# Scaling seven of eight token tiles on VectorE before a plain transpose, and leaving the learned tokens out of the query projections, in one encoder layer on a Trainium2 core

## The chip, the cores and the metric

The program runs on one core of a Trainium2 chip. It uses the core's TensorE (matmuls, in the profile PE, with the weight loads shown apart as PEld), VectorE (DVE), ScalarE (ACT), GpSimd (POOL) and SyncE (SP), which issues nearly all DMAs. The metric is the device time of one execution in microseconds (us); less is better.

## What is computed

The layer takes 1024 tokens of width 1024, puts 16 learned ("meta") tokens in front, and works on 1040 rows. Cut to what the change touches, the reference is:

```python
def rmsnorm(x, w):
    y = xf * lax.rsqrt(jnp.mean(xf * xf, axis=-1, keepdims=True) + RMS_EPS)
    return (y * w)

h = rmsnorm(h_res, norm1_w)                       # 1040 rows
proj = h @ w_in                                   # q | k | v | z | beta, a | sc_b, sc_c, sc_x | gates
o_dn = gated_deltanet_bidir(q, k, v, z, ...)      # conv of 5 taps over tokens on q, k, v; scans both ways
merged = sigmoid(gate_a) * y_a + sigmoid(gate_b) * y_b
h_res = h_res + merged @ w_out
h2 = rmsnorm(h_res, norm2_w)                      # the second norm
gu = h2 @ w_gate_up
h_res = h_res + (silu(gu[..., :D_FF]) * gu[..., D_FF:]) @ w_down
out = rmsnorm(h_res, final_norm_w)[:, N_META:]    # the learned tokens are dropped
```

All of it is float32. A row of the output belongs to one of the 1024 tokens. The learned tokens reach those rows through keys and values of the scans, while a query is used in its own row alone; a query row is a sum of projected rows from two tokens back to two tokens ahead.

## The kernel before, in words

Activations lie transposed, feature by token, so that each weight block of 128 columns can be the stationary operand and the tokens stream past it. To keep float32 accuracy every operand is held as a high and a low part, and a product is three matmuls: high by high, high by low, low by high.

**Stage 1, projections and scans (0 to about 1090 us).** 69 weight blocks of `w_in`, of 128 columns each, are projected as "units" (`u_qkv`, `u_short`, `u_gate`, `u_z`). A unit streams the tokens in chunks through `dense_steps` (lines 287 to 297): 8 steps of 3 matmuls per chunk. `u_qkv(h, i, w)` projects keys (i = 0), queries (i = 1) or values (i = 2) of head h over the chunks `QCH` of 336, 320 and 384 tokens. ACT copies a chunk into the row buffer `raw`, and into `dst` times the middle conv tap. `conv_job` (lines 309 to 326) then adds the other four taps on DVE, in two halves of 520 tokens (`HALF`), with tanh on ACT between. Beside the units run the per-head streams (decay, norm of q and k, triangular inverse, scan), written as generators.

What sets the order in this stage is a planner inside the program: `T` holds a planned time for each engine, `pe(ns)`, `V(n)` and `A(n)` add planned costs as the code is written out, and `run_streams` and `pump` decide by `T` after each dense step which stream or conv step is written next. The order is then fixed; the engines execute it as it stands. A change in any planned cost therefore can move all that is written later in this stage.

**Stage 2 (about 1090 to 1310 us)** is the two branch projections; it is untouched.

**Stage 3, output projection and second norm (about 1310 to 1413 us).** A loop over eight token tiles t of 128 tokens (lines 1261 to 1288). Each does 48 matmuls of 512 columns (`b`, `wh`, `wl`; lines 1273 to 1275), DVE adds the residual (line 1276), ACT squares the row (line 146), DVE makes `rs` = 1/rms in a chain of one-column instructions (`rms_scale`, `rsqrt`), and `hn` = row times norm weight (line 1284; line 1281 for the last tile). `norm_T(t, rs, hn)` then brings the tile to feature-by-token form. It is called one iteration late, so that TensorE does another tile's 48 matmuls in between; the last tile's call comes after the first matmuls of stage 4. In `norm_T`, `hn` is the stationary operand and `diag`, the identity times `rs`, is the moving one: the matmul (line 166) transposes and scales at once. Eight such matmuls a tile; ACT and DVE then split the result into the operands of stage 4 (`b_hl`, and for tiles 4 to 7 sums and differences `m32`, in rows called `al`).

Outside stage 1 a scheduler orders each engine's queue when the program is built.

**Stage 4, the feed-forward (about 1397 us to the end)**: a two-by-two block scheme with seven products in place of eight, called `product` (lines 1333 to 1335). Its moving operands T2 (in rows `mA`), T3, T4 and B22 (in rows `b`) are split at its start by lines 86 and 87 from the results of stage 3, some in a piece of 3 tiles (1536 elements) and a piece of 1 tile.

Of the kernel before, what the change touches and what calls it, by code (L numbers as in the profile page):

```python
# [8 lines left out]
F32 = mybir.dt.float32  # L9
# [3 lines left out]
ALU = mybir.AluOpType  # L13
# [3 lines left out]
P = 128  # L17
D = 1024
KT = 8
SEQ = 1024  # L20
META = 16
# [16 lines left out]
def encoder_layer(ctx: ExitStack, tc: tile.TileContext, x, meta, norm1_w, w_in,  # L38
                  dn_conv_w, A_log, dt_bias, dn_norm_w, sc_conv_w, w_bdn, w_bsc,
                  w_out, norm2_w, w_gu, w_down, final_w, out):  # L40
    nc = tc.nc
    x, out = x[0], out[0]
# [12 lines left out]
    def uid(s):  # L55
        cnt["n"] += 1
        return f"{s}_{cnt['n']}"

    def s4(n=1024):
        return tp.tile([P, 1024], F32, tag="s4", name=uid("s4"), bufs=4)[:, :n]  # L60

    def psm():
        return ps.tile([P, 512], F32, tag="m", name=uid("pm"), bufs=3)

    def psd():
        return ps.tile([P, 512], F32, tag="e", name=uid("pe"), bufs=2)
# [6 lines left out]
    def psany():  # L73
        rot["i"] += 1
        return (psm, psm, psm, psd, psd, pss, pss, pss)[rot["i"] % 8]()

    ident = keep.tile([P, P], F32, name="ident")
    make_identity(nc, ident)

    mm = nc.tensor.matmul  # L80

    def transpose(dst, src, n=P):
        nc.tensor.transpose(dst, src, ident[:n, :n])

    def split(hi, lo, src):
        nc.scalar.copy(hi, src)  # L86
        nc.vector.tensor_tensor(out=lo, in0=src, in1=hi.bitcast(F32), op=ALU.subtract)  # L87
# [64 lines left out]
    def sub(out, a, b):  # L152
        nc.vector.tensor_tensor(out=out, in0=a, in1=b, op=ALU.subtract)

    def norm_T(t, rs, hn):

        diag = tp.tile([P, P], F32, tag="diag", name=uid("diag"), bufs=1)
        nc.vector.tensor_scalar(out=diag, in0=ident, scalar1=rs, scalar2=None, op0=ALU.mult)
        c = slice(t % 4 * P, t % 4 * P + P)
        pts = []  # L160
        for g in range(2):
            pt = psany().rearrange("p (k t) -> p k t", k=4)
            pts.append(pt)
            for k in range(4):
                kk = 4 * g + k
                mm(pt[:, k], hn[:, kk * P:(kk + 1) * P], diag, start=True, stop=True)
            if t < 4:
                split(*(m[:, :, c] for m in mov[("B11", "B21")[g]]), pt)
        if t < 4:
            return  # L170
        b11h, b11l = (m[:, :, c].bitcast(F32) for m in mov["B11"])
        b22, t1, t2, t3 = (m[:, :, c] for m in m32)
        nc.scalar.copy(b22, pts[1])
        sub(t1, pts[0], b11h)
        sub(t1, t1, b11l)
        sub(t2, b22, t1)
        sub(t3, b22, pts[0])
# [34 lines left out]

    HALF = ((0, 520), (520, 520))
    QCH = ((0, 336), (336, 320), (656, 384))

# [5 lines left out]
    def on(e, ns, ready=0.0):  # L223

        T[e] = max(T[e], ready, T["pe"]) + ns
        return T[e] + TOPE
# [5 lines left out]
    def V(n, kind=0):  # L232
        return on("dve", (68 + 1.042 * n, 130 + 1.042 * n, 130 + 0.52 * n)[kind])

    def A(n):
        return on("act", 144 + 0.834 * n)
# [19 lines left out]
    def enqueue(lane, gen):  # L256
        j = Job(gen)
        if not lanes[lane]:
            spent[lane] = max(spent[lane], min(spent.values()))
        lanes[lane].append(j)  # L260
        return j
# [26 lines left out]
    def dense_steps(po, w, xx, t0, n):  # L288
        wh, wl = w
        xh, xl = xx  # L290
        t0 += C0
        for k in range(KT):
            mm(po[:, :n], wh[:, k], xh[:, k, t0:t0 + n], start=(k == 0), stop=False)  # L293
            mm(po[:, :n], wh[:, k], xl[k][:, t0:t0 + n], start=False, stop=False)  # L294
            mm(po[:, :n], wl[:, k], xh[:, k, t0:t0 + n], start=False, stop=(k == KT - 1))  # L295
            pe(3 * (n / 2.4 + 13))
            yield
# [3 lines left out]
    def row_buffer():  # L301
        if len(raws) >= 2:
            force(raws[-2])
        return d1.tile([P, 1044], F32, tag="ra", name=uid("ra"), bufs=2)

    def half_buffer():
        return d1.tile([P, 520], F32, tag="rb", name=uid("rb"), bufs=3)

    def conv_job(raw, dst, col, st_, key):

        for h0, hn in HALF:
            acc = dst[:, h0:h0 + hn]
            while st_["rows"] < h0 + hn + 4:
                yield max(T["pe"], T["dve"]) + 300
            for t in (0, 1, 3, 4):
                nc.vector.scalar_tensor_tensor(out=acc, in0=raw[:, h0 + t:h0 + t + hn], scalar=wc[:, t, col:col + 1],  # L316
                                               in1=acc, op0=ALU.mult, op1=ALU.add)
                V(hn, 1)
                yield T["dve"] + DEP
            th = half_buffer()  # L320
            nc.scalar.activation(th[:, :hn], acc, AF.Tanh)
            on("act", 0, T["dve"] + HOP)
            yield A(hn)
            nc.vector.scalar_tensor_tensor(out=acc, in0=th[:, :hn], scalar=1.0, in1=acc, op0=ALU.add, op1=ALU.mult)
            t = V(hn, 1)
        yield t

    def u_qkv(h, i, w):

        st_ = heads[h]  # L330
        if i == 0:
            st_["kq"] = d1.tile([P, 2, L], F32, tag="kq", name=uid("kq"), bufs=3)
            st_["vT"] = d1.tile([P, L], F32, tag="vT", name=uid("vT"), bufs=2)
        col = (8 + h, h, 16 + h)[i]
        dst = (st_["kq"][:, 0], st_["kq"][:, 1], st_["vT"])[i]
        raw = None
        sub = {"rows": 0}
        for ci, (t0, n) in enumerate(QCH):
            po = psm()
            yield from dense_steps(po, w, hx, t0, n)  # L340
            if raw is None:
                raw = row_buffer()
                nc.gpsimd.memset(raw[:, 0:2], 0.0)
                nc.gpsimd.memset(raw[:, L + 2:L + 4], 0.0)
            nc.scalar.copy(raw[:, 2 + t0:2 + t0 + n], po[:, :n])
            nc.scalar.activation(dst[:, t0:t0 + n], po[:, :n], AF.Copy, scale=wc[:, 2, col:col + 1])  # L346
            A(n)
            A(n)
            sub["rows"] = 2 + t0 + n if ci < 2 else L + 4
            if ci == 1:  # L350
                job = enqueue("conv", conv_job(raw, dst, col, sub, "t"))
                raws.append(job)
        key = ("tk", "tq", "tv")[i]

        def watch():
            return job.done
        st_[key] = watch
# [580 lines left out]
    with tc.tile_pool(name="st", bufs=1) as st:  # L938
# [6 lines left out]
        raw = st.tile([P, KT, 32], F32, name="wba_raw")  # L945
        rows = st.tile([P, 2, P], F32, name="rows")
        wc = c1.tile([P, 5, 24], F32, name="wc")
        for ts, ci in (((0,), None), ((1, 2), 0), ((3, 4, 5), 1), ((6, 7, 8), 2)):
# [5 lines left out]
            for i, t in enumerate(ts):  # L954
                p = P if t < 8 else META
                xr = xs[t] = st.tile([P, D], F32, tag="xr", name=uid("xr"), bufs=9)
# [10 lines left out]
            if ci == 0:  # L967
# [8 lines left out]
                pt = psd()  # L976
                transpose(pt[:, :120], rows[:120, 0], 120)
                nc.scalar.mul(wc.rearrange("p k t -> p (k t)"), pt[:, :120], 0.5)
                pt = psd()
# [3 lines left out]
            for i, t in enumerate(ts):  # L983
                p = P if t < 8 else META
                hn = xs[t]
                nc.vector.scalar_tensor_tensor(out=hn[:p], in0=hn[:p], scalar=ss[:p, 1, i:i + 1], in1=w1row[:p],
                                               op0=ALU.mult, op1=ALU.mult)
                for g in range(2):
                    pt = psany().rearrange("p (k t) -> p k t", k=4)
                    for k in range(4):  # L990
                        kk = 4 * g + k
# [7 lines left out]
            if ci is None:  # L999
                continue  # L1000
            t0, n = QCH[ci]
            if ci == 1:
# [34 lines left out]
        for d in range(2):  # L1037
            h0 = d * 64
            oth = 64 - h0
            nc.gpsimd.tensor_scalar(out=U2[d][h0:h0 + 64], in0=U[d][h0:h0 + 64], scalar1=-1.0,  # L1040
                                    scalar2=None, op0=ALU.add)
# [141 lines left out]
    tp = ctx.enter_context(tc.tile_pool(name="tp", bufs=1))  # L1183
# [54 lines left out]
    for j in range(KT):  # L1238
# [10 lines left out]
        raw = s4(D)  # L1249
# [3 lines left out]
    wrow = big("w2", [P, D], F32)  # L1253
# [9 lines left out]
    for t in range(KT):  # L1263
        mh, ml = wtiles([P, KT, P])
        for i in range(2):
            split(mh[:, 4 * i:4 * i + 4], ml[:, 4 * i:4 * i + 4], mg[i][:, :, t * P:(t + 1) * P])
        xr = s4(D)
        nc.sync.dma_start(xr, x[t * P:(t + 1) * P])
        for n in range(2):
            po = psany()  # L1270
            sl = slice(512 * n, 512 * n + 512)
            for k in range(KT):
                mm(po, mh[:, k], woh[k][:, sl], start=(k == 0), stop=False)
                mm(po, mh[:, k], wol[k][:, sl], start=False, stop=False)
                mm(po, ml[:, k], woh[k][:, sl], start=False, stop=(k == KT - 1))
            nc.vector.scalar_tensor_tensor(out=xr[:, sl], in0=po, scalar=0.5, in1=xr[:, sl], op0=ALU.mult, op1=ALU.add)
        nc.sync.dma_start(xn_d[t], xr)
        hn = s4(D)
        last = t == KT - 1
        if last:  # L1280
            nc.vector.tensor_tensor(out=hn, in0=xr, in1=wrow, op=ALU.mult)
        rs = rms_scale(keep, xr, P, "ss2", s4(D) if last else hn)
        if not last:
            nc.vector.tensor_tensor(out=hn, in0=xr, in1=wrow, op=ALU.mult)
        if t:
            norm_T(*late_norm)
        late_norm = t, rs, hn
# [101 lines left out]
    for j in range(NF):  # L1389
# [9 lines left out]
        if j >= HK:  # L1399
            k = j - HK  # L1400
# [157 lines left out]
```

## Time and profile before

| | before |
|---|---|
| median of 3 runs | 2044.15 us (2043.72 to 2045.39) |
| profiled execution, first to last instruction (span) | 2041.3 us |
| PE busy, share of the span | 2003.0 us, 98% |
| DVE, ACT, POOL busy | 1412.3, 790.9, 109.1 us |
| weight loads (PEld) busy | 1745.0 us |
| mean granted TensorE clock | 0.998 |

The profile gives the profiled execution's time as its span. The timed runs count what lies around it too, so the median stands 2.85 us above the span. Durations of matmuls overlap (they are pipelined), so the cost of one is read from the distance between starts.

### The profile page before, as it was taken

To read this page: it belongs to the slowest core of one execution; us is meant where nothing else is said; L and a number is where in the kernel's file an instruction comes from. 1 tells how busy PE (TensorE), PEld (TensorE's weight loads), DVE (VectorE), ACT (ScalarE), POOL (GpSimd) and SP (SyncE) were. 2 spreads that over 40 slices of the span, in tenths; PEclk is the share of its full clock that TensorE was granted. 3 is DMA by queue.
4 is the path that set the end of the run, shared out by engine and by line. 5 is a ranking of instruction groups with operands and counts; after the bars stand their busy time and mean duration, and the time that the engine had idled before them with its cause. 6 is when DMAs were issued, how large, how long until landed. Compare 5 with 4: busy or idle time off the path is not lost.

```text
span 2041.3 us, 32116 instructions
## 1 busy us (share of the span) xinstructions
PE 2003.0 (98%) x12075; PEld 1745.0 (85%) x12075; DVE 1412.3 (69%) x3129; ACT 790.9 (39%) x1873; POOL 109.1 (5%) x392
## 2 busy tenths in 40 slices
PE   6999999999999999999999999999999999999998
PEld 6999899999999898978888888888888888888886
DVE  6789486887977686856445534458978778756576
ACT  5363235454544554453334211124323223224343
POOL 0002110202020020201000000000000000000000
PEclk9999999999999999999999999999999999999999
DMA  4122312222222213132326734122766355487654
GB/s 140 42 85 68 74 59 62 79 63 58 73 58 81 81 58 94 57 89 78 97 70 200 255 114 142 53 83 93 238 226 221 125 180 168 153 277 247 195 176 155
DMA packets 250722, 248.40 MB, mean 122 GB/s; under 512 B 46084, under 2 KB 190773, under 8 KB 248133
## 3 DMA queue, kind: packets, MB, share of 16 engines
q1 hardware_dynamic: 250565, 246.34, 38.6%
q8 instruction: 95, 1.56, 0.3%
q14 instruction: 62, 0.51, 0.1%
HBM read 179.62 MB, written 66.67 MB: 121 GB/s over the span
## 4 chain that ended last, share of the span: by engine, by line
PE 81%; DVE 11%; ACT 3%; DMA 1%; issue 1%; SPq 0%; ACTq 0%; DVEq 0%
PE pm L293 9%; PE pm L295 9%; PE pm L294 9%; PE pm L1335 3%; PE pm L1334 3%; PE pm L1333 3%; PE pd L1334 2%; PE pd L1335 2%; PE pd L1333 2%; DVE kq L316 2%; PE pe L1335 2%; PE pe L1334 2%; PE pe L1333 2%; PE pd L771 1%; PE pd L119 1%; PE pd L121 1%
## 5 line engine op out<-in xcount | busy, mean ns | idle before, releaser
L293 PE MATMUL pm<-hTh,wh 128*128 128x512 f32 (+4 forms) x1424 | 525.8, 369 | 2.0 <-ACT wh L896 1.0
L295 PE MATMUL pm<-hTh,wl 128*128 128x512 f32 (+4 forms) x1424 | 490.1, 344 | 0.2
L294 PE MATMUL pm<-al,wh 128*128 128x512 f32 (+4 forms) x1424 | 488.9, 343 | 0.3 <-DVE al L998 0.3
L293 PEld LDWEIGHTS pm<-hTh,wh 128*128 128x128 f32 x1424 | 268.4, 189 | 21.7 <-issue 2.7
L295 PEld LDWEIGHTS pm<-hTh,wl 128*128 128x128 f32 x1424 | 267.4, 188 | 20.9 <-DVE wl L893 1.2
L294 PEld LDWEIGHTS pm<-al,wh 128*128 128x128 f32 x1424 | 268.7, 189 | 15.4 <-DVE al L998 0.7
L87 DVE TENSOR_TENSOR al<-raw,ring_h 128x1024 fp32r<-128x1024 f32 x73 | 88.3, 1222 | 64.7 <-ACT ring_h L86 64.3
L893 DVE TENSOR_TENSOR wl<-raw,wh 128x512 fp32r<-128x512 f32 x134 | 90.5, 686 | 50.8 <-ACT wh L896 50.2
L86 ACT CAST ring_h<-raw 128x1024 fp32r<-128x1024 f32 x73 | 76.7, 1055 | 105.7 <-PE pe L1478 34.8
L316 DVE SCALAR_TENSOR_TENSOR kq<-ra,wc,kq 128x520 f32<-128x520 f32 x128 | 97.4, 761 | 5.3 <-ACT kq L346 3.9
L86 ACT CAST wh<-raw 128x1024 fp32r<-128x1024 f32 x45 | 47.4, 1053 | 123.0 <-issue 29.9
L896 ACT CAST wh<-raw 128x512 fp32r<-128x512 f32 x134 | 78.8, 618 | 9.7 <-PE pm L294 9.6
L778 ACT ACTIVATE w<-pd,small 128x128 f32<-128x128 f32 x128 | 40.0, 365 | 105.0 <-PE pd L771 85.7
L452 DVE TENSOR_TENSOR fP<-fP,tm 128x135 f32<-128x135 f32 (+23 forms) x248 | 72.2, 291 | 4.9
L448 DVE TENSOR_TENSOR tm<-fP,fN 128x135 f32<-128x135 f32 (+23 forms) x248 | 72.2, 291 | 4.2
L1337 DVE TENSOR_TENSOR b<-pm,b 128x512 f32<-128x512 f32 x67 | 45.1, 686 | 33.5 <-PE pm L1335 31.1
L800 DVE SCALAR_TENSOR_TENSOR S<-S,eGl,pd 128x128 f32<-128x128 f32 x104 | 31.8, 344 | 46.6 <-PE pd L788 29.4
L87 DVE TENSOR_TENSOR wl<-raw,wh 128x1024 fp32r<-128x1024 f32 x45 | 54.9, 1219 | 9.2 <-ACT wh L86 9.1
L617 POOL TENSOR_TENSOR tm<-mP,mN 1x15 f32<-1x15 f32 (+7 forms) x120 | 42.2, 352 | 274.2 <-DMA mN<-ndm 265.7
L1337 DVE TENSOR_TENSOR b<-pd,b 128x512 f32<-128x512 f32 x54 | 36.5, 686 | 22.2 <-PE pd L1335 22.2
L316 DVE SCALAR_TENSOR_TENSOR vT<-ra,wc,vT 128x520 f32<-128x520 f32 x64 | 48.3, 755 | 2.6 <-ACT vT L346 1.1
L486 ACT ACTIVATE PQ<-PQ,negG 128x128 f32<-128x128 f32 x128 | 43.2, 394 | 15.7 <-DVE PQ L481 15.6
(623 smaller groups left out, 4649.3 us busy)
## 6 DMA issues: line engine op xcount, KB each, us to landing
raw<-in_w_in_dram SPq DMA_DIRECT2D x72, 512.0 KB
raw<-in_w_gate_up_dram SPq DMA_DIRECT2D x44, 512.0 KB
sums<-in_w_down_dram SPq DMA_DIRECT2D x22, 512.0 KB
t_d<-sums SPq DMA_DIRECT2D x11, 1024.0 KB
raw<-s_d SPq DMA_DIRECT2D x44, 256.0 KB
raw<-t_d SPq DMA_DIRECT2D x44, 256.0 KB
act_d<-b SPq DMA_DIRECT2D x43, 256.0 KB
raw<-act_d SPq DMA_DIRECT2D x33, 256.0 KB
```

The costliest lines, as they stand in the source:

```text
L86: nc.scalar.copy(hi, src)
L87: nc.vector.tensor_tensor(out=lo, in0=src, in1=hi.bitcast(F32), op=ALU.subtract)
L293: mm(po[:, :n], wh[:, k], xh[:, k, t0:t0 + n], start=(k == 0), stop=False)
L294: mm(po[:, :n], wh[:, k], xl[k][:, t0:t0 + n], start=False, stop=False)
L295: mm(po[:, :n], wl[:, k], xh[:, k, t0:t0 + n], start=False, stop=(k == KT - 1))
L316: nc.vector.scalar_tensor_tensor(out=acc, in0=raw[:, h0 + t:h0 + t + hn], scalar=wc[:, t, col:col + 1], in1=acc, op0=ALU.mult, op1=ALU.add)
L893: nc.vector.tensor_tensor(out=u[1][1][:, k], in0=u[2][:, k], in1=u[1][0][:, k].bitcast(F32), op=ALU.subtract)
L896: nc.scalar.copy(u[1][0][:, k], u[2][:, k])
L1333: mm(po, ah[:, k], bhk, start=k == 0, stop=False)
L1334: mm(po, ah[:, k], blk, start=False, stop=False)
L1335: mm(po, al[:, k], bhk, start=False, stop=k == 3)
L1337: add = lambda out, a, b: nc.vector.tensor_tensor(out=out, in0=a, in1=b, op=ALU.add)
```

## The change

Three things, in one diff:

1. In the second norm, tiles 0 to 6 get `rs` on VectorE: line 1284 becomes one instruction that multiplies the row by `rs` and by the weights. `norm_T` no longer makes `diag` for them and calls TensorE's transpose (the helper on line 83, with the constant identity) in place of the matmul. Tile 7 stays as it was.
2. Query units stream 322 instead of 336 tokens in their first chunk (tokens 14 to 335; the 16 learned tokens are 0 to 15, and the conv reaches two back). The memset of the left border is dropped for queries.
3. The conv of a query starts at token 16: its first half has 504 columns instead of 520, in five DVE instructions and one of ACT. The planner's costs follow.

```diff
     def norm_T(t, rs, hn):
-        diag = tp.tile([P, P], F32, tag="diag", name=uid("diag"), bufs=1)
-        nc.vector.tensor_scalar(out=diag, in0=ident, scalar1=rs, scalar2=None, op0=ALU.mult)
+        if t == KT - 1:
+            diag = tp.tile([P, P], F32, tag="diag", name=uid("diag"), bufs=1)
+            nc.vector.tensor_scalar(out=diag, in0=ident, scalar1=rs, scalar2=None, op0=ALU.mult)
...
-                mm(pt[:, k], hn[:, kk * P:(kk + 1) * P], diag, start=True, stop=True)
+                if t == KT - 1:
+                    mm(pt[:, k], hn[:, kk * P:(kk + 1) * P], diag, start=True, stop=True)
+                else:
+                    transpose(pt[:, k], hn[:, kk * P:(kk + 1) * P])
...
+    QUERY = ((14, 322), *QCH[1:])
...
-    def conv_job(raw, dst, col, st_, key):
-        for h0, hn in HALF:
+    def conv_job(raw, dst, col, st_, first):
+        for h0, hn in ((first, 520 - first), HALF[1]):
...
-        for ci, (t0, n) in enumerate(QCH):
+        for ci, (t0, n) in enumerate(QUERY if i == 1 else QCH):
...
-                nc.gpsimd.memset(raw[:, 0:2], 0.0)
+                if i != 1:
+                    nc.gpsimd.memset(raw[:, 0:2], 0.0)
...
-                job = enqueue("conv", conv_job(raw, dst, col, sub, "t"))
+                job = enqueue("conv", conv_job(raw, dst, col, sub, META if i == 1 else 0))
...
         if not last:
-            nc.vector.tensor_tensor(out=hn, in0=xr, in1=wrow, op=ALU.mult)
+            nc.vector.scalar_tensor_tensor(out=hn, in0=xr, scalar=rs, in1=wrow, op0=ALU.mult, op1=ALU.mult)
```

Line numbers of the changed program run up to 6 higher than before; numbers behind a buffer's name differ too.

TensorE's queue in stage 3, at the first tile that is transposed (`pd` is the PSUM bank, `s` the tile `hn`), before:

```order
L1275 MATMUL pe_14168<-b_2224_13522,wl_14135 128x512
L166 MATMUL pd_14211<-diag_14209,s_2292_14120 128x128 x4
L166 MATMUL pd_14218<-diag_14209,s_2292_14120 128x128 x4
L1273 MATMUL pd_14233<-b_2223_13521,wh_14225 128x512
L1274 MATMUL pd_14233<-b_2225_13523,wh_14225 128x512
```

and of the change:

```order
L1281 MATMUL pe_14160<-b_2224_13514,wl_14127 128x512
L83 MATMUL pd_14201<-ident,s_2292_14112 128x128 x4
L83 MATMUL pd_14208<-ident,s_2292_14112 128x128 x4
L1279 MATMUL pd_14223<-b_2223_13513,wh_14215 128x512
L1280 MATMUL pd_14223<-b_2225_13515,wh_14215 128x512
```

Nothing moved there; eight matmuls became eight transposes. From stage 2 to the first products of stage 4 this is TensorE's only difference.

VectorE's queue behind the last tile's residual, up to the `diag` that the last tile's transposing matmuls wait for (`ss` is the one-column chain of `rs`, `mA` and `b` with 4x384 the splits of T2 and T3, L1337 an addition of stage 4), before:

```order
L134 SCALAR_TENSOR_TENSOR ss_2361_14746<-ss_2361_14746 128x1
L87 TENSOR_TENSOR b_2374_14844<-al_14058,b_2374_14844 128x4x384
L135 SCALAR_TENSOR_TENSOR ss_2361_14746<-ss_2361_14746 128x1
L87 TENSOR_TENSOR mA_14833<-al_14057,mA_14833 128x4x384
L134 SCALAR_TENSOR_TENSOR ss_2361_14746<-ss_2361_14746 128x1
L153 TENSOR_TENSOR al_14057<-b_hl,al_14057 128x4x384
L135 SCALAR_TENSOR_TENSOR ss_2361_14746<-ss_2361_14746 128x1
L1337 TENSOR_TENSOR b_2373_14843<-pm_14865,b_2373_14843 128x512
L185 TENSOR_TENSOR al_14057<-al_14057,b_hl 128x4x384
L1337 TENSOR_TENSOR b_2373_14843<-pm_14902,b_2373_14843 128x512
L158 TENSOR_SCALAR diag_14917<-ident,ss_2361_14746 128x128
```

and of the change:

```order
L135 SCALAR_TENSOR_TENSOR ss_2355_14726<-ss_2355_14726 128x1
L87 TENSOR_TENSOR mA_14811<-al_14049,mA_14811 128x4x384
L134 SCALAR_TENSOR_TENSOR ss_2355_14726<-ss_2355_14726 128x1
L153 TENSOR_TENSOR al_14049<-b_hl,al_14049 128x4x384
L135 SCALAR_TENSOR_TENSOR ss_2355_14726<-ss_2355_14726 128x1
L1343 TENSOR_TENSOR b_2366_14821<-pm_14843,b_2366_14821 128x512
L134 SCALAR_TENSOR_TENSOR ss_2355_14726<-ss_2355_14726 128x1
L189 TENSOR_TENSOR al_14049<-al_14049,b_hl 128x4x384
L135 SCALAR_TENSOR_TENSOR ss_2355_14726<-ss_2355_14726 128x1
L1343 TENSOR_TENSOR b_2366_14821<-pm_14880,b_2366_14821 128x512
L159 TENSOR_SCALAR diag_14895<-ident,ss_2355_14726 128x128
```

One split of 1536 elements that stood ahead of `diag` now stands behind it. Another of the three big splits of `b` (that of B22) moves from ahead of the last piece of `mA` to behind it.

TensorE's queue in stage 1, where the key-by-query products of head 0 (`L542`, later `L548`) first stand among the dense steps, before:

```order
L294 MATMUL pm_1426<-al_123,wh_1202 128x320
L295 MATMUL pm_1426<-hTh,wl_1203 128x320
L542 MATMUL pe_1457<-kq_245 128x256
L293 MATMUL pm_1426<-hTh,wh_1202 128x320
L294 MATMUL pm_1426<-al_123,wh_1202 128x320
L295 MATMUL pm_1426<-hTh,wl_1203 128x320
L293 MATMUL pm_1465<-hTh,wh_1202 128x384
```

and of the change:

```order
L298 MATMUL pm_1460<-hTh,wh_1198 128x384
L299 MATMUL pm_1460<-al_121,wh_1198 128x384
L300 MATMUL pm_1460<-hTh,wl_1199 128x384
L548 MATMUL pe_1467<-kq_245 128x256
L298 MATMUL pm_1460<-hTh,wh_1198 128x384
L299 MATMUL pm_1460<-al_121,wh_1198 128x384
```

The product stands 9 matmuls later, in the next chunk. From here on the streams of stage 1 stand a few dense steps earlier or later than before. The units themselves keep their sequence, and after the last scan's last transposes 15 matmuls of dense steps are left in this stage where 27 were.

## The prediction

> **What bounds the kernel now.** I read the page first (busy times, the slices, the chain that ended last), then busy time by stage, then the waits of TensorE, and last the timeline at each place that the change touches.
>
> ```profile
> span 2041.3 us, 32116 instructions
> PE 2003.0 (98%) x12075; PEld 1745.0 (85%) x12075; DVE 1412.3 (69%) x3129; ACT 790.9 (39%) x1873; POOL 109.1 (5%) x392
> PE   6999999999999999999999999999999999999998
> DVE  6789486887977686856445534458978778756576
> PE 81%; DVE 11%; ACT 3%; DMA 1%; issue 1%; SPq 0%; ACTq 0%; DVEq 0%
> ```
>
> TensorE is busy in every slice but the first and the last, and 81% of the chain that ended last is its own work. So time taken off TensorE's instructions should come off the span, unless another engine holds TensorE up where the time was saved. The views by stage say where that could be.
>
> ```profile
> 1310.00:1397.00 87.00, 87.00 (x438) 73.94 (x437) 49.02 (x130) 22.09 (x39) 0.00 (x0) 1.00 0.31 103
> 1397.00:1444.00 47.00, 45.15 (x212) 37.18 (x211) 46.55 (x71) 25.76 (x33) 0.00 (x0) 1.00 0.31 105
> ```
>
> The columns are length, then busy time of PE, PEld, DVE, ACT and POOL, the granted clock, DMA share and GB/s. In the output projection with the second norm, TensorE is busy 87.00 of 87 us, at clock 1.00, and DVE 49. In the 47 us after it, DVE is busy 46.55 and TensorE loses 1.85: there DVE bounds the time. Most of the change lies in the first stretch and one piece of it on the border.
>
> ```profile
> DVE s L1276 <- PE pe L1275: 20.5, 6, 4.7
> DVE s L1276 <- PE pm L1275: 20.3, 5, 4.7
> ```
>
> In that stretch DVE waits for TensorE (over 40 us in all) and not the other way.
>
> **Part 1, seven tiles transposed plainly.** The old way, and what a plain transpose costs where the kernel has one already:
>
> ```profile
> 1319.88 0.39 PE L1275 MATMUL pe<-b,wl 128*128 128x512 f32 x1
> 1320.11 1.95 PE L166 MATMUL pd<-diag,s 128*128 128x128 f32 x16
> 1321.81 0.48 PE L1273 MATMUL pd<-b,wh 128*128 128x512 f32 x1
> 1322.13 0.40 PE L1274 MATMUL pd<-b,wh 128*128 128x512 f32 x1
> ...
> 1083.91 0.60 PE L83 MATMUL pd<-ident,NP 128*128 128x128 f32 x4
> 1084.26 0.48 PE L293 MATMUL pm<-hTh,wh 128*128 128x512 f32 x1
> 1084.58 0.40 PE L294 MATMUL pm<-al,wh 128*128 128x512 f32 x1
> ```
>
> A 512-column matmul starts 0.23 us after the one before it (1320.11 less 1319.88). The program has eight matmuls for a tile; the trace has 16 records, two passes each. They hold TensorE from 1320.11 to 1321.81 and delay the next start by another 0.09 (0.32 instead of 0.23): 1.79 us, 0.112 a pass. Four transposes in the queue of the scans, one record each, take 0.35 and delay by the same 0.09: 0.44, or 0.11 each. So a transpose costs one pass where the float32 matmul costs two: 8 x 0.11 = 0.88, and a tile saves 1.79 - 0.88 = **0.91 us**. Six tiles (0 to 5) lie wholly in the stretch where TensorE never waits: 6 x 0.91 = **5.5 us**.
>
> [...]
>
> Slow transposes do exist in this trace, when TensorE has just sat idle; this is the other bound:
>
> ```profile
> 10.11 1.94 PE L83 MATMUL pm<-ident,xr 128*128 128x128 f32 x8 [10.11 <-DVE xr L986]
> 11.84 0.68 PE L83 MATMUL pe<-ident,rows 120*128 120x120 f32 x2
> ```
>
> Eight take 1.73 us there (11.84 less 10.11). At that rate a tile saves 0.06 and seven save 0.4. I take 0.11, since in stage 3 TensorE comes from 48 matmuls without a gap.
>
> What pays for it on DVE: line 1284 becomes an instruction with a scalar, which the first norm has already.
>
> ```profile
> L1284 DVE TENSOR_TENSOR s<-s,w x7: 1215/1216/1217, 1311.5 to 1385.8; 128x1024 f32<-128x1024 f32 x7
> L986 DVE SCALAR_TENSOR_TENSOR xr<-xr,ss,w1row x9: 1267/1280/1285, 8.7 to 38.1; 128x1024 f32<-128x1024 f32 x8, 16x1024 f32<-16x1024 f32 x1
> L158 DVE TENSOR_SCALAR diag<-ident,ss x8: 277/288/289, 1314.4 to 1411.1; 128x128 f32<-128x128 f32 x8
> ```
>
> That is 64 ns more and 288 ns less a tile: DVE gains 0.22. It adds a wait, since the row now needs `rs` first. Behind it in DVE's queue stand only the next tile's residuals (line 1276), which wait for TensorE anyway (rows above); and the tile's transposes come 5 us later:
>
> ```profile
> 1338.96 0.29 DVE L158 TENSOR_SCALAR diag<-ident,ss 128x128 f32<-128x128 f32 x1
> ...
> 1345.47 1.95 PE L166 MATMUL pd<-diag,s 128*128 128x128 f32 x16
> ```
>
> `diag` was made at 1338.96; the scaled row will start about 1.2 us earlier (its old product no longer stands ahead of the chain) and end near 1339.1, for a use at 1345. I cost it at nothing. Cover gone, it would cost at most one such instruction a tile, 7 x 1.28 = 9 us.
>
> **Part 2, the border.** Tile 6's transposes come after the last residual, at the start of the stretch that DVE bounds.
>
> ```profile
> 1396.39 0.69 DVE L1276 SCALAR_TENSOR_TENSOR s<-pe,s 128x512 f32<-128x512 f32 x1 [4.75 <-PE pe L1275]
> ...
> 1402.97 1.75 DVE L87 TENSOR_TENSOR b<-al,b 128x1536 fp32r<-128x1536 f32 x1
> 1404.64 0.15 DVE L135 SCALAR_TENSOR_TENSOR ss<-ss 128x1 f32<-128x1 f32 x1
> ...
> 1411.12 0.28 DVE L158 TENSOR_SCALAR diag<-ident,ss 128x128 f32<-128x128 f32 x1
> ...
> 1411.45 2.05 PE L166 MATMUL pe<-diag,s 128*128 128x128 f32 x16 [1.51 <-DVE diag L158]
> ...
> 1419.13 0.50 PE L1334 MATMUL pd<-mA,mB 128*128 128x512 f32 x1 [0.34 <-DVE mA L87]
> ...
> 1429.69 0.39 PE L1334 MATMUL pe<-b,mB 128*128 128x512 f32 x1
> ```
>
> From the residual at 1396.39 DVE works without a gap to `diag` at 1411.12, and TensorE waits 1.51 us for it. If DVE's queue were the same, tile 6's 0.91 would only lengthen that wait: gain 0. But the order shows a split of 1536 elements, 1.67 us (1402.97 to 1404.64), moved from ahead of `diag` to behind it, and another from ahead of the last piece of `mA` to behind it, so both things TensorE waits for come 1.67 us sooner. TensorE arrives 0.91 sooner, so its wait falls from 1.51 to about 0.75. Gain between 0 and **1.67 us**; I take 1.67, as the moved instruction has a row of its own. What is late next is the deferred split of B22; the product that reads its low part starts at 1429.69, 10.6 us after the `mA` piece, so I see nothing behind it.
>
> **Part 3, 14 columns fewer.** 8 heads x 24 matmuls.
>
> ```profile
> L294 PE MATMUL pm<-al,wh 128*128 128x336 f32 x176 | 55.9, 318 | 0.0
> L294 PE MATMUL pm<-al,wh 128*128 128x322 f32 x128 | 40.0, 312 | 0.0
> ```
>
> Line 294 at 336 columns against 322 (the short conv's units have that chunk already): 6 ns. 8 x 24 x 6 ns = 1.15 us; head 0's run at the start, where TensorE waits for the first norm, so seven heads count: **1.0 us**. DVE and ACT save a little off the path; POOL's eight memsets set nothing that TensorE waits for.
>
> **Part 4, the replanned stage 1.** The cheaper costs move everything the planner writes from head 0's norm on. What that can gain or lose is bounded by TensorE's waits there now:
>
> ```profile
> PE pe L542 <- DVE PQ L571: 2.9, 5, 0.9
> PE pe L83 <- DVE Nm L525: 2.1, 4, 0.9
> PE pe L1120 <- DVE gc L1114: 1.9, 1, 1.9
> PE pm L293 <- ACT wh L896: 1.0, 1, 1.0
> PE pd L771 <- DVE r L766: 0.4, 2, 0.3
> ```
>
> 8.3 us between 60 and 1090 us, in 13 places. All gone is -8.3; twice as many is +8.3. They are chance meetings of a full DVE queue with a bank or operand, and a new order draws them anew, so I take 0 and keep -3 to +4 for the range (a third gone; half as many again). At the stage's end 15 matmuls of dense steps instead of 27 still stand behind the last scan, so no tail is laid bare. SyncE's queue moves along in this stage by a place or two; its weight loads keep their sequence, and in stage 4 a few loads and stores change places with a neighbour.
>
> **Sum**: 5.5 + 1.67 + 1.0 = 8.2 us off the span of 2041.3, so 2033.1. The runs' median stands 2.85 us above that span (2044.15), so I predict **2036.0 us**, 0.40% less. About 0.2%, 4.1 us, is what a measurement of this kernel can tell from no change.
>
> **Rivals.**
> - *Stage 1 gives the gain back*: the new order adds waits of 4 to 8 us. For: every stream moved; DVE is over 80% busy in several slices. Against: same units, same kinds of instruction. Time 2040 to 2044.
> - *Slower than before*: the key-by-query product (line 542) needs a bank that DVE releases, and there are 64 of them. Now 5 wait, 0.58 us each. If the moved ones mostly stood ahead of DVE's release, each would wait that long; the gain is eaten from 14 more waits, and with 26 more (15 us) the time is 2051. Against: the planner holds a product back by the same rule as before.
> - *DVE binds at the border*: the queue runs differently from what I read and the 1.67 and another 0.9 are given back: 2038.5.
> - *Transposes run at the cold rate*, whatever the clock row says: 0.4 + 1.0 us, with 1.67 at the border: 2041.1. [...]
> - *The change does not do what it says*: the order shows transposes from tile 0 on, and 322 columns; only the time of a pass could disappoint.
>
> **How the numbers follow.** Forecast 0.72 (2033 to 2039.5); stage 1 gives back 0.14; DVE at the border 0.07; cold transposes 0.02; slower by line 542 0.05. Range 2032.5 to 2041: stage 1's -3 and +4 with the border's 0 to 1.67. The forecast and the border case are faster by over 0.2% (below 2040.1), with a little of the first rival: 0.79. Within 0.2%: 0.16. Slower by over 0.2%: 0.05.
>
> **What would show it.** The tiles follow each other now at a distance that two rows give:
>
> ```profile
> L166 PE MATMUL pd<-diag,s x64: 270/275/275, 1320.1 to 1397.9; 128*128 128x128 f32 x64
> L166 PE MATMUL pm<-diag,s x48: 270/275/275, 1332.8 to 1385.2; 128*128 128x128 f32 x48
> ```
>
> In the changed profile: 56 transposes of `s`, eight about 1.04 us long as a merged row, and the next start 0.88 after the first; tile pitch 11.8 instead of 12.7 us (from 1320.1 to 1332.8, first starts); TensorE still busy through the stage; the wait for `diag` near 0.75 and for `mA` near 0.3; TensorE's waits between 60 and 1090 near 8.3 us. A sum of those waits over 12 us, or a new wait between 1400 and 1444, would make the prediction wrong.

## The result and the profile after

| | before | after |
|---|---|---|
| median, first measurement | 2044.77 us (2043.72 to 2046.32, 4 runs) | 2035.14 us (2034.40 to 2036.20, 4 runs) |
| ratio, 95% interval | | 0.9952 (0.9940 to 0.9964) |
| median, measured again in a later group | 2045.30 us (9 runs) | 2035.74 us (5 runs), ratio 0.9956 (0.9944 to 0.9969) |
| profiled execution, span | 2041.3 us | 2033.1 us (timed 2034.81) |

The change makes the kernel 9.6 us faster. Forecast were 2036.0 us and a gain of 8.2 us.

The page of the changed kernel, the lines that answer to those of before:

```profile
span 2033.1 us, 31988 instructions
PE 1997.2 (98%) x12019; PEld 1739.7 (86%) x12019; DVE 1409.5 (69%) x3122; ACT 792.0 (39%) x1873; POOL 110.0 (5%) x384
PE   6999999999999999999999999999999999999998
PE 70%; DVE 5%; ACT 1%; issue 0%; DMA 0%; SPq 0%; ACTq 0%; DVEq 0%
```

TensorE is as full as before and does 5.8 us less (2003.0 to 1997.2). The last row, the chain that ended last, is not comparable with that of before: its shares add up to 76% here and to 97% there, since it is followed back only to about 480 us. The stretches of stage 3 and of the border to stage 4, by the view of busy time (length, then PE, PEld, DVE, ACT, POOL, granted clock):

```profile
1310.00:1390.00 80.00, 80.00 (x379) 66.75 (x378) 47.51 (x120) 20.53 (x38) 0.00 (x0) 1.00 0.34 112
1390.00:1436.00 46.00, 45.01 (x210) 37.06 (x209) 45.61 (x69) 25.73 (x32) 0.00 (x0) 1.00 0.30 101
```

TensorE still never waits in the output projection, so what was taken off it there came off the time. At the border it loses 0.99 us where it lost 1.85.

The first transposed tile, in the timeline (start, length, then the instruction), and the start of the next tile's transposes:

```profile
1319.05 0.39 PE L1281 MATMUL pe<-b,wl 128*128 128x512 f32 x1
1319.28 1.03 PE L83 MATMUL pd<-ident,s 128*128 128x128 f32 x8
1320.07 0.48 PE L1279 MATMUL pd<-b,wh 128*128 128x512 f32 x1
1320.38 0.40 PE L1280 MATMUL pd<-b,wh 128*128 128x512 f32 x1
...
1331.05 1.03 PE L83 MATMUL pm<-ident,s 128*128 128x128 f32 x8
```

Eight records of one pass where there were sixteen. They hold TensorE for 0.79 us (1319.28 to 1320.07) and delay the next start by 0.08 (0.31 for 0.23): 0.87, where 0.88 was forecast. The tiles follow each other at 11.77 us (1319.28 to 1331.05).

The groups of instructions (count, then busy time, mean ns of one, idle time before):

```profile
L83 PE MATMUL pd<-ident,s 128*128 128x128 f32 x32 | 4.1, 272 | 0.0
L83 PE MATMUL pm<-ident,s 128*128 128x128 f32 x24 | 3.1, 272 | 0.0
L1290 DVE SCALAR_TENSOR_TENSOR s<-s,ss,w 128x1024 f32<-128x1024 f32 x7 | 9.0, 1284 | 0.2
```

These are 56 transposes that wait for nothing. The scaled row costs DVE 1284 ns, and no TensorE instruction of the stage waits for one.

DVE's timeline over the border, from the last residual to `diag`:

```profile
1390.12 0.69 DVE L1282 SCALAR_TENSOR_TENSOR s<-pe,s 128x512 f32<-128x512 f32 x1 [4.09 <-PE pe L1281]
...
1396.44 1.75 DVE L87 TENSOR_TENSOR mA<-al,mA 128x1536 fp32r<-128x1536 f32 x1
...
1403.04 0.28 DVE L159 TENSOR_SCALAR diag<-ident,ss 128x128 f32<-128x128 f32 x1
...
1405.18 1.75 DVE L87 TENSOR_TENSOR b<-al,b 128x1536 fp32r<-128x1536 f32 x1
```

and TensorE's waits there (total, times, longest):

```profile
PE pe L168 <- DVE diag L159: 0.6, 1, 0.6
PE pd L1340 <- DVE mA L87: 0.4, 1, 0.4
```

No split of `b` of 1536 elements stands ahead of `diag` any more; the first starts at 1405.18, behind it, where one started at 1402.97, ahead of it, before. From residual to `diag` DVE takes 12.92 us where it took 14.73, and TensorE's wait is 0.6 where it was 1.51. No new wait came up.

TensorE's waits in stage 1, between 60 and 1090 us:

```profile
PE pe L1126 <- DVE gc L1120: 2.0, 1, 2.0
PE pe L83 <- DVE Nm L531: 1.6, 2, 1.0
PE pe L548 <- DVE PQ L577: 1.3, 2, 1.2
PE pm L298 <- ACT wh L902: 1.0, 1, 1.0
PE pd L777 <- DVE r L772: 0.9, 3, 0.5
```

With three more of 0.2 to 0.3 they sum to 7.5 us in 12 places; 8.3 in 13 places before.

### The profile page after: what moved, and what is told of

It is laid out like the page before. It is cut to its first block, busy times and chain, and to the rows that moved or that the text cites. A ratio compares the mean times of both kernels' runs of the same rounds, so it can differ in the third digit from the quotient of the medians.

```text
span 2033.1 us, 31988 instructions
## 1 busy us (share of the span) xinstructions
PE 1997.2 (98%) x12019; PEld 1739.7 (86%) x12019; DVE 1409.5 (69%) x3122; ACT 792.0 (39%) x1873; POOL 110.0 (5%) x384
## 4 chain that ended last, share of the span: by engine, by line
PE 70%; DVE 5%; ACT 1%; issue 0%; DMA 0%; SPq 0%; ACTq 0%; DVEq 0%
PE pm L298 6%; PE pm L300 6%; PE pm L299 6%; PE pm L1341 3%; PE pm L1340 3%; PE pm L1339 3%; PE pd L1340 2%; PE pd L1341 2%; PE pd L1339 2%; PE pe L1341 2%; PE pe L1340 2%; PE pe L1339 2%; PE pd L119 1%; PE pd L121 1%; PE pd L120 1%; PE pm L1483 1%
## 5 line engine op out<-in xcount | busy, mean ns | idle before, releaser
L321 DVE SCALAR_TENSOR_TENSOR kq<-ra,wc,kq 128x520 f32<-128x520 f32 (+1 forms) x128 | 96.4, 753 | 7.7 <-ACT kq L352 6.2
```

## The experiments

Two theories stood against each other from the start. Mine: the second norm's part gives 7.2 us by fewer passes of TensorE (5.5) and a shorter DVE queue ahead of `diag` (1.67); the query's part gives 1.0 by columns, and the new order of stage 1 gives nothing. The rival: the border or the queue gives nothing, and the rest comes from the new order. Eleven kernels, the whole change among them, were timed in three groups, each group beside runs of the kernel before on the same chip; differences below are against those (2045.27, 2045.56 and 2045.30 us).

### The two parts apart

`norm_only` has the norm part and the old query units:

```diff
-    QUERY = ((14, 322), *QCH[1:])
...
-        for h0, hn in ((first, 520 - first), HALF[1]):
+        for h0, hn in HALF:
...
-        for ci, (t0, n) in enumerate(QUERY if i == 1 else QCH):
+        for ci, (t0, n) in enumerate(QCH):
```

> The program before with the second norm's part of the change alone; queries keep 336 columns and the old plan. Its order from the output projection on is that of the changed kernel. Theory (the terms add): 6 tiles x 0.91 us = 5.5 us on TensorE and 1.67 us at the border from the moved split, so 7.2 us less than before (about 2037.6 beside 2044.8); stage 1 ends where it did before. Rival (the gain comes mostly from the replanned stage 1): less than 5 us.

2038.40 us, ratio 0.9969 (0.9958 to 0.9979): 6.9 us faster than before.

`query_only` is the other half, with the norm as before:

```diff
-                    transpose(pt[:, k], hn[:, kk * P:(kk + 1) * P])
+                    mm(pt[:, k], hn[:, kk * P:(kk + 1) * P], diag, start=True, stop=True)
...
-            nc.vector.scalar_tensor_tensor(out=hn, in0=xr, scalar=rs, in1=wrow, op0=ALU.mult, op1=ALU.mult)
+            nc.vector.tensor_tensor(out=hn, in0=xr, in1=wrow, op=ALU.mult)
```

> The query part alone, with the planner following it; the second norm as before. Theory: 1.0 us from the columns, and the stage's waits drawn anew, which were 8.3 us before and 7.5 us in the changed kernel: 1 to 2 us less than before. Rival (the changed kernel's missing 1.4 us between its span's 8.2 and its median's 9.6 us lies here): 2.5 us or more.

2042.11 us, ratio 0.9985 (0.9976 to 0.9995): 3.2 us faster, by its interval 1.0 to 4.9. The halves add up to 10.1, the whole is 9.6. The norm part is near its 7.2 (interval 4.3 to 8.6); the query part is above its 1.0.

### Order and columns of stage 1

`plan_only` computes all columns and gives the planner the cheaper costs; `cols_old_plan` leaves the columns out and gives it the old ones:

```diff
     def dense_steps(po, w, xx, t0, n, plan=None):
-            pe(3 * (n / 2.4 + 13))
+            pe(3 * ((plan or n) / 2.4 + 13))
...
+            pn = n - 14 if i == 1 and ci == 0 else n
-            yield from dense_steps(po, w, hx, t0, n)
+            yield from dense_steps(po, w, hx, t0, n, pn)
```

(with `n + 14` in the second kernel, and the conv's planned costs likewise).

> Nothing is left out of the work (336 columns, conv of 520), but the planner is told the costs of the shortened query: the order of stage 1 is that of the changed kernel on TensorE, VectorE, ScalarE and SyncE, with the old work. Theory (a new order only draws the waits anew): within 1 us of before, waits of TensorE between 60 and 1090 us 7 to 9 us. Rival (the new order is better or worse by itself): 2 us or more either way.

> The shortened query (322 columns, conv from token 16) in the old order: the planner is told the old costs. Theory: seven heads x 24 matmuls x 6 ns = 1.0 us less than before, the waits of stage 1 as before (8.3 us), and the start (head 0) unchanged. Rival (a saved column only lengthens a wait): 0.

2042.93 us (0.9989, 0.9979 to 0.9998) and 2043.51 us (0.9992, 0.9982 to 1.0001): 2.3 and 1.8 us faster, with intervals of about 2 us to each side. The same two edits on top of the norm part, five rounds, with the whole change beside them:

> The norm part together with the planner's cheaper costs, with all query columns computed as before. Theory as predicted (order 0, columns 1.0 us): about 1.0 us slower than the whole change run again beside it, 7.2 us faster than before. Rival (order worth 1.5 to 2.5 us, columns 0.5 to 1): 0.5 to 1 us slower than the whole change, and 1 to 2 us faster than the run with the norm part and the columns under the old order.

> The norm part of the change together with the 14 columns fewer, while the planner of stage 1 is given the old costs, so that stage 1 is written in the order of before. Theory as predicted (a new order of stage 1 is worth 0; columns 1.0 us; norm part 7.2 us): the time of the whole change run again beside it, within 0.7 us. Rival (the new order is worth 1.5 to 2.5 us, as the run with the new order alone came out): 1.5 to 2.5 us slower than the whole change.

> The whole change unaltered, as the one that the other three of this call are compared with on the same chip. Theory as predicted: 9.6 us faster than before, within 0.7 us, as its first measurement was. If the first measurement had luck: 7 to 9 us faster.

| | norm before | norm changed |
|---|---|---|
| old order, all columns | 0 | -6.9 |
| new order, all columns | -2.3 | -7.8 |
| old order, fewer columns | -1.8 | -8.0 |
| both | -3.2 | -9.6 |

(us against the kernel before of the same group). `norm_plan` took 2037.54 us, `norm_cols` 2037.33, the whole change 2035.74. The order is worth 0.9 to 2.3 us by the four differences of the table, the columns 0.9 to 1.8; together 2.7 to 3.2, where I had 1.0. Each value is uncertain by about 2 us or a little more, so the medians do not tell how these 3 us divide between the two.

The traces do. I take the distance from the first matmul of `al,wba`, behind the slow start, to the first of stage 2 (line 119), and take off what half clock cost in between: 1.7 us for each stretch (last section). The kernel before, without a stretch, and `plan_only`, with one:

```profile
26.36 0.47 PE L1018 MATMUL pe<-al,wba 128*32 128x336 f32 x2
1091.63 0.39 PE L119 MATMUL pe<-hTh,wh 128*128 128x512 f32 x1
```

```profile
27.33 0.46 PE L1020 MATMUL pe<-al,wba 128*32 128x336 f32 x2
1091.81 0.39 PE L119 MATMUL pe<-hTh,wh 128*128 128x512 f32 x1
```

| length of stage 1, us | norm before | norm changed |
|---|---|---|
| old order, all columns | 1065.28 | 1065.05 |
| new order, all columns | 1062.77 | 1063.52 |
| old order, fewer columns | 1064.27 | 1064.11 |
| both | 1062.70 | 1062.35 and 1062.65 |

There is one profile for each kernel and two for the whole change. The five other profiles with both lie between 1062.5 and 1062.8. Under the old order the columns give 0.9 and 1.0 us, as forecast; under the new one 0.1 to 1.2. The order gives 1.5 to 2.5 us, where I had 0, and both together 2.4 to 2.7. TensorE's waits between 60 and 1090 us explain a part of the order's gain: 8.3 to 8.7 us in the four profiles with the old order, 7.4 to 8.0 in the five with the new one. Where the rest comes from stays open.

The norm part reads as clearly. From the first matmul of the output projection to the first of the last matmul stage (1298.35 to 1821.14 before; lines 1273 and 1476) TensorE takes 522.8 us in the four kernels with the old norm and 515.6 to 516.1 in the five profiles with the new one: 6.7 to 7.2 us less, for a forecast of 7.2.

### Is it the passes of TensorE?

`ident_matmul` keeps the scaled row and puts the ordinary float32 matmul by the identity in place of the transpose; `transpose_twice` does each transpose two times. In both, the scheduler puts the split of `b` ahead of `diag` again, so the border's gain should go with the passes. In both profiles the wait for `diag` is back at 1.5 us.

```diff
-                    transpose(pt[:, k], hn[:, kk * P:(kk + 1) * P])
+                    mm(pt[:, k], hn[:, kk * P:(kk + 1) * P], ident, start=True, stop=True)
```

```diff
-                    transpose(pt[:, k], hn[:, kk * P:(kk + 1) * P])
+                    for _ in range(2):
+                        transpose(pt[:, k], hn[:, kk * P:(kk + 1) * P])
```

> The changed kernel, but tiles 0 to 6, scaled by VectorE, are multiplied by the constant identity as ordinary float32 matmuls instead of transposed. In its order the split of 1536 elements stands ahead of diag again, as before the change. Theory (the gain is the second pass of TensorE and the moved split, none of it VectorE's scaling): 5.5 + 1.67 = 7.2 us more than the changed kernel, tile pitch 12.7 us. Rival (the scaling on VectorE is itself worth something): 5 us more or less than that.

> The changed kernel with each plain transpose of tiles 0 to 6 done twice into the same place: twice the transposes, nothing else. Here too the split stands ahead of diag again. Theory (a transpose costs one pass, 0.11 us, at the full clock): 6 x 8 x 0.11 = 5.3 us and 1.67 us at the border, 7.0 us more than the changed kernel. [...]

2042.30 us (0.9982, 0.9973 to 0.9991) and 2042.50 us (0.9986, 0.9976 to 0.9996): 3.3 and 3.1 us faster than before, which is the query part alone. The timeline of `ident_matmul` at the first tile:

```profile
1319.22 1.95 PE L170 MATMUL pd<-ident,s 128*128 128x128 f32 x16
1320.92 0.48 PE L1279 MATMUL pd<-b,wh 128*128 128x512 f32 x1
1321.23 0.40 PE L1280 MATMUL pd<-b,wh 128*128 128x512 f32 x1
```

and of `transpose_twice`:

```profile
1318.56 1.91 PE L83 MATMUL pd<-ident,s 128*128 128x128 f32 x16
1320.22 0.48 PE L1280 MATMUL pd<-b,wh 128*128 128x512 f32 x1
```

The matmul by the identity is back at 16 passes and 1.70 us to the next start, though DVE scales the row and no `diag` is made. Sixteen transposes take 1.66 us to the next start. What the change saves in these tiles is passes: with them back the whole gain of the norm part is gone (from the output projection to the last matmul stage 522.8 and 522.6 us, 522.8 before), so the row scaled on DVE neither gains nor costs anything that can be seen here.

The length of a record is not its cost. One transpose's record lasts 272 ns in the changed kernel, while sixteen transposes here take 1.66 us to the next start, 0.10 each.

### What bounds the border?

`t3_first` writes the first split of T3 ahead of the last tile's transposes, so that two splits of 1536 elements stand ahead of `diag` in DVE's queue:

```diff
+    split(*(m[:, :, 0:384] for m in mov["T3"]), m32[3][:, :, 0:384])
     norm_T(*late_norm)
...
+            if n == "T3" and c.start == 0:
+                continue
```

> The changed kernel with one piece of code moved: the split of T3's first three tiles is written ahead of the last tile's norm. VectorE's queue then has two splits of 1536 elements ahead of diag instead of none, and one of 512 less: 2 x 1.67 - 0.6 = 2.7 us more. TensorE's work is the same. Theory (VectorE's queue sets the border): the wait for diag grows from 0.6 to about 3.3 us and the time by 2.7 to 4 us. Rival (TensorE alone counts, or the wait is made up by shorter waits behind it): under 1 us.

2038.98 us, ratio 0.9970 (0.9961 to 0.9980): 6.6 us faster than before, so 3.0 of the whole change's 9.6 are lost (each uncertain by about 2 us). TensorE's waits and then its timeline at that place:

```profile
PE pe L168 <- DVE diag L159: 3.4, 1, 3.4
```

```profile
1406.70 3.50 PE L168 MATMUL pe<-diag,s 128*128 128x128 f32 x16 [3.36 <-DVE diag L159]
1409.96 0.48 PE L1341 MATMUL pd<-b_hl,wl 128*128 128x512 f32 x1
```

and DVE's timeline, the last residual and `diag`:

```profile
1390.71 0.69 DVE L1282 SCALAR_TENSOR_TENSOR s<-pe,s 128x512 f32<-128x512 f32 x1 [4.09 <-PE pe L1281]
...
1406.37 0.28 DVE L159 TENSOR_SCALAR diag<-ident,ss 128x128 f32<-128x128 f32 x1
```

The wait grows from 0.6 to 3.4 us, and DVE's way from the last residual to `diag` from 12.92 to 15.66 us. DVE's queue does bound the border, and what stands ahead of `diag` is paid for there. In this execution TensorE paid again behind the wait: the 16 passes took 3.26 us to the next start, 0.20 each, as eight did at the program's start (1.73), and the granted clock was lower:

```profile
1406.50:1412.00 5.50, 5.30 (x25) 4.95 (x26) 5.46 (x8) 1.73 (x3) 0.00 (x0) 0.70 0.33 95
```

This profiled execution was the slowest of the kernel's nine (2041.73 us). From the output projection to the last matmul stage it takes 519.1 us, the whole change 515.6 and 515.9: 3.2 to 3.5 more, of which 1.5 is half clock (it began at 1406.35, shortly before the wait ended). Without it the place costs 1.7 to 2.0 us in this trace, near the 2.4 by which the waits for `diag` and `mA` together grew (2.74 more for `diag`, 0.37 less for `mA`). How many of the other executions paid the half clock too is not known.

`eight_plain` treats the last tile like the others: no `diag` at all.

```diff
-        if t == KT - 1:
+        if False:
             diag = tp.tile([P, P], F32, tag="diag", name=uid("diag"), bufs=1)
...
-        if last:
-            nc.vector.tensor_tensor(out=hn, in0=xr, in1=wrow, op=ALU.mult)
-        rs = rms_scale(keep, xr, P, "ss2", s4(D) if last else hn)
-        if not last:
+        rs = rms_scale(keep, xr, P, "ss2", hn)
+        if True:
             nc.vector.scalar_tensor_tensor(out=hn, in0=xr, scalar=rs, in1=wrow, op0=ALU.mult, op1=ALU.mult)
```

> The changed kernel with the last tile scaled by VectorE and transposed plainly as well, so diag is gone. TensorE does 0.91 us less. VectorE loses two instructions (1.14 and 0.28 us) and gets one of 1.28 us behind the chain of rs, and the scheduler puts one split of 1536 elements ahead of it. Theory (VectorE sets the border): no gain, 0 to 1.5 us more than the changed kernel, with TensorE waiting some 2 us for the scaled row. Rival (TensorE bounds here too): 0.9 us less.

> The kernel in which the last tile too is scaled by VectorE and transposed plainly, unaltered, with more rounds. If TensorE bounds the last tile's place: 0.9 us faster than the whole change run again beside it (eight matmuls of 1.79 us for eight transposes of 0.88). If VectorE's queue bounds it (the scaled row of 1.28 us takes the place of the 0.28 us product): 0 to 1.0 us slower.

2034.53 us at first (0.9949, 0.9934 to 0.9964), 11.0 us faster than before in a group without the whole change; then 2035.58 beside 2035.74 of the whole change. The medians show no difference, but would not surely show 0.9 us either (five runs each, 2034.41 to 2037.65 and 2035.01 to 2037.56). Its wait at the border, DVE's timeline there, and TensorE's:

```profile
PE pe L83 <- DVE s L1288: 1.6, 1, 1.6
```

```profile
1402.88 1.27 DVE L1288 SCALAR_TENSOR_TENSOR s<-s,ss,w 128x1024 f32<-128x1024 f32 x1
1404.07 1.22 DVE L87 TENSOR_TENSOR wl<-raw,wh 128x1024 fp32r<-128x1024 f32 x1
```

```profile
1404.20 1.09 PE L83 MATMUL pe<-ident,s 128*128 128x128 f32 x8 [1.62 <-DVE s L1288]
1405.34 0.51 PE L1339 MATMUL pd<-b_hl,wl 128*128 128x512 f32 x1
```

TensorE is done with the transposes after 1.14 us, and it waited 1.0 us longer for them: the 1.27 us of the scaled row stand in the place of the 0.28 us of `diag`. The transposes save 0.67 us (1.14 for 1.81), the later wait for `mA` of 0.37 is gone, and the added wait of 1.0 takes both back. From the output projection to the last matmul stage both profiles of this kernel take 515.5 us, the whole change 515.6 and 515.9. So at this place an exchange of TensorE's time for DVE's brought nothing.

## Why the prediction was right

**Part 1, six tiles, 5.5 us: right.** From the first transposes to the last residual TensorE needs 70.84 us (1319.28 to 1390.12) where it needed 76.28 (1320.11 to 1396.39): 5.44. The two kernels that bring the passes back lose this part and the border's, as they must. The rival of transposes at half the rate fell with the same rows.

**Part 2, the border, 1.67 us: right.** From the residual to `diag` DVE takes 1.81 us less. The forecast of the wait was 0.75 and it is 0.62; the wait for `mA` is 0.37 for a forecast of 0.3. What went late, the split of B22, delays nothing. `t3_first` shows that the queue ahead of `diag` was the cause. The norm part measured alone gives 6.9 us for 7.2, and by the other three rows of the table of medians 5.5 to 6.4, each uncertain by more than this gap; by the distance in the traces it is 6.7 to 7.2.

**Part 3, columns 1.0: right under the old order.** There stage 1 is 0.9 and 1.0 us shorter; under the new one the three differences are 0.1 to 1.2.

**Part 4, order 0: the term that was wrong.** The new order takes 1.5 to 2.5 us off stage 1. The prediction counted only on waits drawn anew and took nothing for them. They fell, from 8.3 to 7.5 us in the first profile (those for the bank of the key-by-query product from 2.9 to 1.3), but the order gains more than that, and what else it gains is not known. Neither the rival in which stage 1 gives the gain back nor the slower one came.

**The sum, 8.2 us, was too small for that reason.** By the traces the norm part gives 6.7 to 7.2 us and the query part 2.4 to 2.7, together 9.1 to 9.9; the medians say 9.6. The interval of the 9.6 alone (7.4 to 12.3 us) would hold 8.2 too. The range's ends do not follow from the terms named for them: 3 below the forecast and 4 + 1.67 above it are 2033.0 and 2041.6, where 2032.5 and 2041 stand.

**The span, 2033.1 us: met by luck to a tenth.** The profiled execution after holds 1.7 us of half clock that the one before does not (last section). Without it the two spans differ by 9.9 us, in the second profile of the change by 9.0, where I had summed 8.2. The half clock hid what the new order of stage 1 had gained beyond the sum.

**The step from span to time, +2.85 us.** The run with the profile took 2034.81 us at a span of 2033.1, so 1.7 us lie around the span; the other 1.1 were what the profiled execution of before lay under its median. The step was right for a gain between medians and wrong for a single execution. Result and forecast differ by 0.9 us: 1.5 of gain more than I had, less 0.6 by which the median of before rose with a fourth run.

## What to carry to other kernels

In these traces a float32 matmul that only transposes costs TensorE two passes (eight take 1.79 us), a transpose costs one (0.87). A diagonal that scales on the way can go to VectorE where VectorE has room before the tile's next use, as in tiles 0 to 5; at the border, in the last tile, it earned nothing. What such a change is worth at a place where another engine bounds is read from that engine's queue: one moved split of 1.67 us gave nearly as much as two transposed tiles. And one profiled execution is one draw: a difference of 1 to 3 us between two spans should be looked for in the clock row before it is looked for in the code, and then in the length of the stage that the change touches. That length told parts of 1 to 2 us apart that ten runs of a kernel could not.

## What the runs showed of the hardware

The granted clock drops to half for short stretches inside the program, in some executions of a kernel and not in others. The view of busy time of the changed kernel, as profiled first:

```profile
45.00:50.00 5.00, 3.88 (x32) 3.39 (x30) 2.94 (x9) 2.71 (x7) 0.00 (x0) 1.00 0.00 0
50.00:55.00 5.00, 5.00 (x21) 5.00 (x21) 0.00 (x0) 0.09 (x1) 0.00 (x0) 0.66 0.01 3
```

and of the kernel before at the same place:

```profile
45.00:50.00 5.00, 3.88 (x31) 3.38 (x30) 2.94 (x9) 2.44 (x7) 0.00 (x0) 1.00 0.02 3
50.00:55.00 5.00, 5.00 (x31) 5.00 (x30) 0.00 (x0) 0.96 (x2) 0.00 (x0) 1.00 0.00 0
```

TensorE is busy all 5 us in both, with 21 matmuls in one and 31 in the other. The clock of 0.66 over 5 us is 1.7 us lost, which at half speed is a stretch of 3.4 us: the clock is 0.50 from 49.98 to 53.39 us. The whole change profiled again does not have it there, and has one at 98 us, behind a wait that the kernel before has too (1.9 us) without one:

```profile
97.14 0.41 PE L1126 MATMUL pe<-gc,U2f 128*128 128x72 f32 x2 [2.04 <-DVE gc L1120]
...
98.57 0.52 PE L300 MATMUL pm<-hTh,wl 128*128 128x384 f32 x1
98.89 0.52 PE L298 MATMUL pm<-hTh,wh 128*128 128x384 f32 x1
99.21 0.52 PE L299 MATMUL pm<-al,wh 128*128 128x384 f32 x1
```

Starts of 384-column matmuls lie 0.32 us apart there, and 0.17 to 0.18 ahead of the wait (93.90, 94.07, 94.24, 94.42). Over the fourteen profiles such stretches, ahead of the program's end, cost 0 us (the kernel before and `query_only`), 1.7 (nine profiles), 3.4 (two) or 5.1 (`t3_first`: three, one of them at the long wait at the border). They begin at 49 to 50 us, 97 to 101 us, 1833 to 1839 us and, in `t3_first`, at 1406 us. So the spans of these profiles differ by steps of 1.7 us, and by one more wait in code that the change leaves alone: that for `ring_h` near 1830 us takes 0.2 to 2.1 us in the fourteen profiles. The profiled execution of before had none, which fits its median's 1.1 us above span and surroundings.

The length of the wait ahead of a stretch does not tell whether one comes. The wait for `gc` near 98 us takes 1.9 to 2.0 us in all fourteen profiles; eight have a stretch there and six have none. In the two profiles of the whole change it is 2.04 us with a stretch and 2.02 without:

```profile
98.85 0.41 PE L1126 MATMUL pe<-gc,U2f 128*128 128x72 f32 x2 [2.02 <-DVE gc L1120]
```

It is 1.90 us both in `norm_plan`, where the starts of 384-column matmuls go from 0.17 to 0.32 us apart at 100.7, and in the kernel before, whose clock stays at 1.00 there. Near 50 us TensorE is idle for 1.12 us (0.35 and 0.77) in the changed kernel as profiled first, with a stretch behind it, and for 1.11 us (0.35 and 0.76) in the kernel before, without one. What decides is open.
